# Two mixers reordered: hgrn ahead of attention's projections, output gates late

## The chip, the cores and the metric

One core of one Trainium2 chip. The metric is the device time of one execution in microseconds (us). Times in the profile count from the first instruction of the profiled execution.

## The reference

Two transformer blocks on 512 tokens of width 1024, in float32. The change touches the first block's two layers and a helper that the second block's attention also uses. Each layer of the first block is `x + gate * mixer(norm(x))`, then a SwiGLU. The mixer, cut to what matters:

```
proj = h @ w_in                                   # 1024 -> 2824
out_a = sliding_window_attention(rope(norm(aq)), rope(norm(ak)), av, sinks)       # 8 heads, window 128
out_b = rmsnorm(hgrn2_chunked(bq, log_f(bf), bv)) * silu(bg)                      # gated recurrence, 4 heads
out_c = rmsnorm(gated_delta_chunked(cq, ck, cv, beta, g)) * silu(cg)              # delta net, 4 heads
mixed = concat(out_a, out_b, out_c) @ w_out
```

`aq`, `ak`, ... are slices of `proj`; `cq`, `ck`, `cv` pass a causal convolution of width 4 and a silu first. A vector of modulations, `silu(c) @ ada_w + ada_b`, gives scale, shift and gate of each layer.

## The kernel before, in words

**Order of the work.** The kernel is traced as one straight program. A planner then lays out the queue of each engine by a timeline of its own, in which program order is the priority: work named earlier goes first where both could run. Tiles of one tag share a fixed number of buffers, and buffers are given in program order: a tile waits for the release of the one whose place it takes. Semaphores are put in by the planner. `after` (line 280) adds an order of issue between two instructions, without a wait.

**ScalarE's tables.** `act` (line 263) keeps track of the function table: Exp and Ln share one, Silu has another. When the next function in program order needs the other table, it loads it at that point (line 270), ordered behind all uses of the table before it. So all Exp and Silu uses keep their program order by groups.

**Generators.** Each part of a mixer is a generator that yields between pieces; `run` runs generators to their ends one after the other, `mix` interleaves them by counts, `islice(g, n)` runs n pieces, `track` sets the group of tiles and the PSUM tag of `psm`. This order of naming is the priority. Matrix products go through `mm` (line 297), transposes through `tr` (line 301), activations through `act` (line 274), so most instructions carry these lines, and tiles tell them apart.

**PSUM.** Each mixer has eight banks: two each of tags pd (projections, heads and scores of attention), pg (delta net, transposed probabilities of attention), po (modulation, accumulated values of attention, output rows of the delta net), ph (hgrn).

**A mixer** (function `mixers` in `build`, from line 2090): `mixer` projects keys, values and gate inputs; `gdn_gates` prepares the delta net's decays; `gdn_proj` projects `qT`, `kT`, `vT` with convolution and Silu, then the delta net's output gate `sg` (256 columns by tokens, `gen_tok`) and hgrn's output gate `hg` (256 columns, `run_cm`). Then `run` names, in this order:

- `gdn`: the delta net (`gen_gdn`, line 899). Norms (`csq`, `ln`), decay masks, `AT` and `QK`, an inverse by doubling (`T`, `TT`, `Y`, `Ah`), `kbg`, `kd`, `vb`, `U`, `WT`, a scan of 8 chunks (`St`, `VN`), the output `O`, its norm (`oms`), the product with `sg` (two POOL multiplications and `om`) and transposes into `gout`.
- `ap`: attention's query projection `aq`, two loads of 256 columns. `hp`: hgrn's `hz`, `hq`, `hv`, three loads. A load is 1 MB of weights, split into a high and a low part (ScalarE copies, VectorE subtracts), three matmuls per 128 rows.
- `ada` (layer 0 only): modulations 2 to 5, each four loads of 1 MB and 32 matmuls into one po bank, then transposes in another.
- attention (`gen_attn`, line 1262): squares and rms norm (Ln, Exp in `rsqrt_s`), rope, heads transposed (`gen_heads`), then scores of four blocks (`sm`, `nm`, `den`) mixed with values (`gen_values`, line 1342). The first 18 pieces come alone; the rest is mixed two to one with `part`, the output rows 6 and 7 (those of the delta net) into po.
- `hg_(0)`, `hg_(1)`: hgrn (`gen_hgrn`, line 1103) for two halves of the channels: gates with Exp and Ln (`he`, `lf`), a cumulated sum, seven levels of `ed` against masks into `hW`, the output `hO`, its norm (`hsq`, with Ln and Exp) and the product with `hg`.

Behind the mixer, `mixed` splits the outputs and runs the remaining output rows through `gen_out`.

**Values** (`gen_values`): per key block, probabilities of two groups of four heads are transposed into PSUM, the first group copied by VectorE, the second by ScalarE into `PT`, then two products into the two halves of one po bank:

```
if G:
    self.act(T[G], p)
else:
    self.nc.vector.tensor_copy(T[G], p)
...
for G in range(2):
    g = slice(G * 64, G * 64 + 64)
    self.mm(po[g], V[:, g], T[G], s == 0, s == len(keys) - 1)
```

The third mixer (`even`) calls the same function, with pd, po and pn as banks and six keys in each of four blocks.

Of the kernel before, what the change touches and what calls it, by code (L numbers as in the profile page):

```python
# [168 lines left out]
class Net:  # L169
# [662 lines left out]
    def gdn_proj(self, l, X, Wv):  # L832

        self.grp, self.pg = "G", "pg"
        conv = self.P(f"conv{l}").rearrange("p (c j) -> p c j", j=4)
        qkv = [self.pair([128, 2, 512], n) for n in ("qT", "kT", "vT")]

        def fin(c, p):
            y = self.t([128, 512], "cy")
            self.act(y, p, AF.Copy, scale=conv[:, c, 3:4])  # L840
            for s in (1, 2, 3):
                self.stt(y[:, s:], p[:, :512 - s], conv[:, c, 3 - s:4 - s], y[:, s:], OP.mult, OP.add)
            self.act(qkv[c // 2][:, c % 2], y, AF.Silu)

        self.run_cm(Wv, 1792, 768, X, fin)
        sg = self.pair([128, 2, 2, 4, 64], "sg")

        def fg(b, p):
            v = p.rearrange("p (j h e) -> p h j e", j=2, h=2)
            for hh in range(2):  # L850
                self.act(sg[:, hh, :, b, :], v[:, hh], AF.Silu)

        self.run_tok(X, 4, (Wv[:, :, 2560:2816],), fg)
        self.grp = "P"
        hg = self.pair([128, 2, 512], "hg")
        self.run_cm(Wv, 1536, 256, X, lambda c, p: self.act(hg[:, c], p, AF.Silu))
        return qkv, sg, hg

# [39 lines left out]

    def gen_gdn(self, l, qkv, sg, gates, out):
        nc, g = self.nc, self.nc.gpsimd  # L900
        lb, G, rest, gl = gates
        qT, kT, vT = qkv
# [153 lines left out]
        for hh in range(2):  # L1056
            d = slice(hh * 64, hh * 64 + 64)
            p = self.psm().rearrange("p (u e) -> p u e", e=64)
            for u in range(8):
                q, b = divmod(u, 4)  # L1060
                for j in range(2):
# [4 lines left out]
        yield from sysmm(QK, Pair([v.rearrange("p q b e -> p (q b) e") for v in VN.t]),  # L1066
                         lambda hh, p: self.tt(O[:, hh], O[:, hh], p, OP.add))

        ms = self.t([128, 16], "oms")
        for hh in range(2):  # L1070
# [21 lines left out]
    def gen_hgrn_proj(self, X, Wv, out):  # L1092
        pr = lambda n: self.pair([128, 2, 512], n)
        z, q, vT = pr("hz"), pr("hq"), pr("hv")
        cp = lambda t: (lambda c, p: self.act(t[:, c], p))
        for c0, fn in ((1024, cp(z)), (768, cp(q)), (1280, cp(vT))):
            yield from self.gen_cm(Wv, c0, 256, X, fn)
        out += [z, q, vT]

# [242 lines left out]
    def gen_values(self, b, keys, den, out, pt, pv, py):  # L1342

        po = self.psm(pv)
        for s, (P, o, V) in enumerate(keys):
            T = []
            for G in range(2):
# [4 lines left out]
                if G:  # L1352
                    self.act(T[G], p)
                else:
                    self.nc.vector.tensor_copy(T[G], p)
            for G in range(2):
                g = slice(G * 64, G * 64 + 64)
                self.mm(po[g], V[:, g], T[G], s == 0, s == len(keys) - 1)
            yield
# [681 lines left out]
def build(nc, tc, a, cwhere, pwhere):  # L2041
    with ExitStack() as ctx:
# [20 lines left out]
        for l in range(2):  # L2063
            with ExitStack() as st:
# [25 lines left out]
                def mixers(out, Wov):  # L2090
# [3 lines left out]
                    gates = n.gdn_gates(l, gates)  # L2094
                    qkv, sg, hg = n.gdn_proj(l, X, Wv)
                    proj, qt = [], []
                    T = n.track
                    gdn = T(n.gen_gdn(l, qkv, sg, gates, out), "G", "pg")
                    hp = T(n.gen_hgrn_proj(X, Wv, proj), "P", "pg")
                    ap = T(n.gen_attn_proj(X, Wv, qt), "A", "pg")  # L2100
                    ada = T(chain(*[n.gen_ada_pe(a['ada_w'][0], q, [(c1, n.P('ada_b0'), mods[0])], 'po') for q in (2, 3, 4, 5)]), "A", "pg") if l == 0 else iter(())

                    def hg_(c):
                        yield from T(n.gen_hgrn(l, c, proj + [hg], out), "I", "ph")

# [10 lines left out]
                    part = T(chain(halve(), n.gen_out(Wov, slice(6, 8), Z, col(mods[l], 2), "po", False, 8)), "A", "pg")  # L2116
                    n.run(gdn, ap, hp, ada, chain(islice(at, 18), n.mix((at, 2), (part, 1))), hg_(0), hg_(1))
                    return 6
# [103 lines left out]
```

## Time and profile before

| what | value |
|---|---|
| runs | 3109.3, 3103.52, 3100.19 us; median 3103.52 |
| profiled execution | 3102.67 us, span from first to last instruction 3100.9 us |
| TensorE (PE) busy | 2921.0 us, 94% |
| VectorE (DVE), ScalarE (ACT), GpSimd (POOL) busy | 1422.8, 894.8, 361.4 us |
| granted TensorE clock, mean | 0.949 |
| chain that ended last | PE 85%, DVE 9%, ACT 2%, issue 2%, DMA 1% |

How to read it: PE is busy 94% of the span, so a view of the whole tells little. The granted clock says at which share of its full speed TensorE ran: in each moment one of two levels, 1.0 (2.4 GHz) or 0.5 (1.2 GHz), so a mean between them is a mixture. A matmul at half clock counts as busy for longer. An instruction's `<-` shows which tiles it reads; `[x <-y]` behind a row is idle time of its engine and what ended it.

### The profile page before, as it was taken

The page shows a single profiled execution, that of the slowest core. Times are in us where ns is not written, and L with a number is a line of the kernel's source. Part 1 is how long each engine was busy: PE and PEld are TensorE (multiplying, and loading weights), DVE is VectorE, ACT ScalarE, POOL GpSimd, SP SyncE. Part 2 cuts the span into 40 slices and gives each one's busy share as a digit, 9 for nine tenths or more (in the row PEclk, how much of TensorE's full clock was granted, in tenths as well). Part 3 has the DMA queues.
Part 4 walks back from the last instruction along what each step waited for, and adds up shares of the span by engine and source line. Part 5 has one row for each costly group of instructions (what it writes and reads, how often), then busy time and mean ns, then how long its engine had stood idle before and what let it go on. Part 6 is the DMA issues. An engine that isn't in the chain of part 4 may idle for free.

```text
span 3100.9 us, 42214 instructions
## 1 busy us (share of the span) xinstructions
PE 2921.0 (94%) x17403; PEld 1958.3 (63%) x17403; DVE 1422.8 (46%) x2688; ACT 894.8 (29%) x1716; POOL 361.4 (12%) x284
## 2 busy tenths in 40 slices
PE   7998999999999899999999899899999988999998
PEld 5875578888887667888899744534434474344343
DVE  4346566564546659689545754311111362211112
ACT  4333343233433343423344344211101222011011
POOL 0212111011023202213001300100000011000000
PEclk9996899999999699999999899899999998999998
DMA  6233156563220036599412000899999729999995
GB/s 219 69 119 125 35 151 185 174 188 87 91 65 17 5 102 199 157 300 312 127 58 69 21 21 8 334 409 409 409 409 409 270 83 360 409 389 394 409 409 214
DMA packets 334401, 636.98 MB, mean 205 GB/s; under 512 B 16640, under 2 KB 204288, under 8 KB 334208
## 3 DMA queue, kind: packets, MB, share of 16 engines
q1 hardware_dynamic: 332128, 634.15, 56.4%
q8 instruction: 137, 2.24, 0.3%
q14 instruction: 56, 0.46, 0.0%
q10 hardware_dynamic: 2080, 0.13, 0.0%
HBM read 632.14 MB, written 2.10 MB: 205 GB/s over the span
## 4 chain that ended last, share of the span: by engine, by line
PE 85%; DVE 9%; ACT 2%; issue 2%; DMA 1%; POOL 0%; DVEq 0%; POOLq 0%; ACTq 0%
PE pd L297 41%; PE pm L297 18%; PE pa L297 8%; PE po L297 4%; PE pg L297 4%; PE pe L297 3%; PE pd L301 2%; PE ph L297 2%; DVE aacc L294 1%; PE pn L297 1%; DVE x L294 1%; PE pg L301 1%; DMA raw<-ada_w 1%; DVE rt L285 1%; DVE split L285 1%
## 5 line engine op out<-in xcount | busy, mean ns | idle before, releaser
L297 PE MATMUL pd<-X,split 128*128 128x512 f32 x2640 | 629.8, 394 | 11.4 <-ACT X L274 6.9
L297 PEld LDWEIGHTS pd<-X,split 128*128 128x128 f32 x2640 | 493.4, 189 | 121.6 <-ACT X L274 10.0
L297 PE MATMUL pm<-rawx,xs 128*64 128x512 f32 x1440 | 403.4, 600 | 0.7 <-ACT xs L274 0.5
L297 PEld LDWEIGHTS pm<-rawx,xs 128*64 128x64 f32 x1440 | 126.1, 136 | 190.4 <-issue 180.0
L297 PE MATMUL pa<-rawx,maT 128*64 128x512 f32 x728 | 202.6, 600 | 7.6 <-ACT maT L274 7.6
L274 ACT ACTIVATE split<-raw 128x1024 fp32r<-128x1024 f32 (+5 forms) x164 | 141.9, 871 | 195.6 <-PE pd L297 129.3
L285 DVE TENSOR_TENSOR split<-raw,split 128x1024 fp32r<-128x1024 f32 (+4 forms) x135 | 150.8, 1122 | 87.1 <-ACT split L274 86.2
L297 PE MATMUL pd<-split,X 128*128 128x256 f32 x1296 | 180.1, 293 | 9.4 <-ACT split L274 6.1
L297 PEld LDWEIGHTS pd<-split,X 128*128 128x128 f32 x1296 | 165.3, 195 | 16.0 <-ACT split L274 6.2
L297 PE MATMUL pd<-X,splitx 128*128 128x512 f32 x720 | 173.7, 391 | 0.0
L297 PEld LDWEIGHTS pd<-X,splitx 128*128 128x128 f32 x720 | 135.6, 189 | 29.3
L297 PE MATMUL pd<-aH,split 128*128 128x512 f32 x484 | 153.4, 389 | 0.0
L294 DVE SCALAR_TENSOR_TENSOR x<-pd,modl,x 128x512 f32<-128x512 f32 x136 | 96.5, 746 | 99.5 <-PE pd L297 99.4
L294 DVE SCALAR_TENSOR_TENSOR yL<-pa,gv,yH 128x512 fp32r<-128x512 f32 x32 | 24.0, 750 | 246.5 <-ACT yH L274 246.5
L297 PEld LDWEIGHTS pa<-rawx,maT 128*64 128x64 f32 x728 | 66.6, 137 | 107.5 <-issue 95.9
L1974 DVE COPY gv<-pd 64x1 f32<-64x1 f32 x32 | 5.0, 156 | 272.7 <-PE pd L297 272.5
L285 DVE TENSOR_TENSOR ms<-ms,pm 128x512 f32<-128x512 f32 x32 | 22.0, 688 | 227.5 <-issue 186.9
L294 DVE SCALAR_TENSOR_TENSOR aacc<-rawx,cs_c,aacc 128x512 f32<-128x512 f32 x148 | 125.4, 888 | 0.0
L285 POOL TENSOR_TENSOR aL<-sg,aH 128x512 fp32r<-128x512 f32 x44 | 66.8, 1518 | 398.3 <-ACT aH L274 398.3
L297 PEld LDWEIGHTS pd<-aH,split 128*128 128x128 f32 x484 | 90.9, 188 | 19.4
L274 ACT ACTIVATE split<-rawx 128x1024 fp32r<-128x1024 f32 (+3 forms) x64 | 59.5, 934 | 150.8 <-PE pd L297 122.2
L297 PE MATMUL pm<-raw,xs 128*64 128x512 f32 x272 | 101.5, 597 | 0.0
(683 smaller groups left out, 4738.8 us busy)
## 6 DMA issues: line engine op xcount, KB each, us to landing
rawx<-w_exp_gate SPq DMA_DIRECT2D x94, 1024.0 KB, 14.5
rawx<-w_exp_down SPq DMA_DIRECT2D x91, 1024.0 KB, 12.5
rawx<-w_exp_up SPq DMA_DIRECT2D x86, 1024.0 KB, 17.6
raw<-ada_w SPq DMA_DIRECT2D x30, 1024.0 KB, 5.2
rawx<-w_mod SPq DMA_DIRECT2D x29, 1024.0 KB, 5.4
raw<-w_in SPq DMA_DIRECT2D x22, 1024.0 KB, 5.1
raw<-w_exp_up SPq DMA_DIRECT2D x20, 1024.0 KB, 16.7
raw<-w_mod SPq DMA_DIRECT2D x19, 1024.0 KB, 5.4
```

The costliest lines, as they stand in the source:

```text
L274: i = self.nc.scalar.activation(out, in_, f, **k)
L285: return (eng or self.nc.vector).tensor_tensor(out, a, b, op)
L294: return self.nc.vector.scalar_tensor_tensor(out, a, s, b, op0, op1)
L297: return self.nc.tensor.matmul(out, l, r, start=start, stop=stop, skip_group_check=True)
L301: return self.nc.tensor.transpose(out, x, self.C("ident")[0:k, 0:k])
L1974: nc.vector.tensor_copy(gv[64 * i:64 * i + 64], pg[64 * i:64 * i + 64, i:i + 1])
```

## The change

hgrn's projections take in `hg`, and stand with hgrn's first half right behind the delta net; then come attention's projections, then the gate `sg`, the first 14 pieces of attention, the end of the delta net (`gen_gdn_end`, cut out of `gen_gdn`), then hgrn's second half, the rest of attention and the modulations mixed one to two to two, and the output rows `part` last. In `gen_values` the first product is ordered behind the second group's copy.

```diff
--- before.py
+++ after.py
@@ -843,18 +843,19 @@
             self.act(qkv[c // 2][:, c % 2], y, AF.Silu)
 
         self.run_cm(Wv, 1792, 768, X, fin)
+        return qkv
+
+    def gen_gdn_gate(self, X, Wv, got):
+
         sg = self.pair([128, 2, 2, 4, 64], "sg")
+        got.append(sg)
 
         def fg(b, p):
             v = p.rearrange("p (j h e) -> p h j e", j=2, h=2)
             for hh in range(2):
                 self.act(sg[:, hh, :, b, :], v[:, hh], AF.Silu)
 
-        self.run_tok(X, 4, (Wv[:, :, 2560:2816],), fg)
-        self.grp = "P"
-        hg = self.pair([128, 2, 512], "hg")
-        self.run_cm(Wv, 1536, 256, X, lambda c, p: self.act(hg[:, c], p, AF.Silu))
-        return qkv, sg, hg
+        yield from self.gen_tok(X, 4, (Wv[:, :, 2560:2816],), fg)
 
     def gdn_gates(self, l, gates):
 
@@ -896,7 +897,7 @@
                 self.act(gl[q, j], v(p[:, 32 + 16 * j:48 + 16 * j])[q, hh], AF.Exp)
         return lb, G, rest, gl
 
-    def gen_gdn(self, l, qkv, sg, gates, out):
+    def gen_gdn(self, l, qkv, gates, got):
         nc, g = self.nc, self.nc.gpsimd
         lb, G, rest, gl = gates
         qT, kT, vT = qkv
@@ -1065,7 +1066,11 @@
             yield
         yield from sysmm(QK, Pair([v.rearrange("p q b e -> p (q b) e") for v in VN.t]),
                          lambda hh, p: self.tt(O[:, hh], O[:, hh], p, OP.add))
-
+        got.append(O)
+
+    def gen_gdn_end(self, l, O, sg, out):
+
+        nc, g = self.nc, self.nc.gpsimd
         ms = self.t([128, 16], "oms")
         for hh in range(2):
             sq = self.t([128, 8, 64], "osq")
@@ -1093,9 +1098,10 @@
         pr = lambda n: self.pair([128, 2, 512], n)
         z, q, vT = pr("hz"), pr("hq"), pr("hv")
         cp = lambda t: (lambda c, p: self.act(t[:, c], p))
-        for c0, fn in ((1024, cp(z)), (768, cp(q)), (1280, cp(vT))):
+        hg = pr("hg")
+        for c0, fn in ((1024, cp(z)), (768, cp(q)), (1280, cp(vT)), (1536, lambda c, p: self.act(hg[:, c], p, AF.Silu))):
             yield from self.gen_cm(Wv, c0, 256, X, fn)
-        out += [z, q, vT]
+        out += [z, q, vT, hg]
 
     def gen_hgrn(self, l, c, proj, out):
 
@@ -1350,12 +1356,14 @@
                     self.tr(p[:, j * 128:j * 128 + 128], P[4 * G + j][:, o:o + 128])
                 T.append(self.t([128, 512], "PT"))
                 if G:
-                    self.act(T[G], p)
+                    second = self.act(T[G], p)
                 else:
                     self.nc.vector.tensor_copy(T[G], p)
             for G in range(2):
                 g = slice(G * 64, G * 64 + 64)
-                self.mm(po[g], V[:, g], T[G], s == 0, s == len(keys) - 1)
+                i = self.mm(po[g], V[:, g], T[G], s == 0, s == len(keys) - 1)
+                if G == 0:
+                    self.after(i.ins, second.ins)
             yield
         r = self.t([128, 8], "rden")
         self.nc.vector.reciprocal(r, den)
@@ -2092,16 +2100,20 @@
                     if l == 0:
                         n.consts("a", n.m)
                     gates = n.gdn_gates(l, gates)
-                    qkv, sg, hg = n.gdn_proj(l, X, Wv)
-                    proj, qt = [], []
+                    qkv = n.gdn_proj(l, X, Wv)
+                    proj, qt, O, sg = [], [], [], []
                     T = n.track
-                    gdn = T(n.gen_gdn(l, qkv, sg, gates, out), "G", "pg")
-                    hp = T(n.gen_hgrn_proj(X, Wv, proj), "P", "pg")
-                    ap = T(n.gen_attn_proj(X, Wv, qt), "A", "pg")
+                    gdn = T(n.gen_gdn(l, qkv, gates, O), "G", "pg")
+                    hp = T(n.gen_hgrn_proj(X, Wv, proj), "P", "pd")
+                    ap = T(n.gen_attn_proj(X, Wv, qt), "A", "pd")
+                    sp = T(n.gen_gdn_gate(X, Wv, sg), "G", "pd")
                     ada = T(chain(*[n.gen_ada_pe(a['ada_w'][0], q, [(c1, n.P('ada_b0'), mods[0])], 'po') for q in (2, 3, 4, 5)]), "A", "pg") if l == 0 else iter(())
 
                     def hg_(c):
-                        yield from T(n.gen_hgrn(l, c, proj + [hg], out), "I", "ph")
+                        yield from T(n.gen_hgrn(l, c, proj, out), "I", "ph")
+
+                    def end():
+                        yield from T(n.gen_gdn_end(l, O[0], sg[0], out), "G", "pg")
 
                     BANKS = "pg", "po", "po"
                     at = T(n.gen_attn(l, qt, kv, out, BANKS), "A", "pd")
@@ -2114,7 +2126,7 @@
                             yield
 
                     part = T(chain(halve(), n.gen_out(Wov, slice(6, 8), Z, col(mods[l], 2), "po", False, 8)), "A", "pg")
-                    n.run(gdn, ap, hp, ada, chain(islice(at, 18), n.mix((at, 2), (part, 1))), hg_(0), hg_(1))
+                    n.run(gdn, hp, hg_(0), ap, sp, islice(at, 14), end(), n.mix((hg_(1), 1), (at, 2), (ada, 2)), part)
                     return 6
 
                 mixed(a["w_out"][l], col(mods[l], 2), mixers)
```

## Rows read from the trace of the kernel before

**Rows 1.** Busy time by stretch: start:end, length, PE, PEld, DVE, ACT, POOL, clock, DMA.

```profile
86.60:206.80 120.20, 119.71 (x1482) 104.12 (x1481) 46.91 (x65) 39.66 (x73) 27.93 (x24) 1.00 0.19 63
206.80:319.70 112.90, 95.82 (x1188) 63.41 (x1187) 71.76 (x232) 38.53 (x87) 27.95 (x29) 0.71 0.41 139
319.70:390.60 70.90, 67.70 (x401) 37.16 (x399) 35.40 (x119) 28.01 (x79) 5.34 (x7) 0.85 0.12 38
...
854.60:979.10 124.50, 119.61 (x1419) 103.65 (x1418) 65.26 (x129) 42.63 (x81) 36.82 (x31) 0.99 0.15 48
979.10:1062.10 83.00, 68.75 (x1093) 57.76 (x1092) 57.53 (x167) 33.22 (x74) 20.86 (x22) 0.68 0.02 5
1062.10:1123.90 61.80, 59.30 (x401) 33.48 (x399) 35.20 (x119) 27.60 (x79) 5.35 (x7) 0.90 0.13 43
1807.40:1928.50 121.10, 118.73 (x501) 52.18 (x500) 52.63 (x126) 50.26 (x143) 6.34 (x5) 0.97 0.04 14
```

**Rows 2.** Timeline of PE in the inverse of layer 0: start, length, instruction.

```profile
169.91 2.08 PE L297 MATMUL pg<-Y,TT 64*64 64x64 f32 x64
171.93 2.79 PE L297 MATMUL pd<-X,split 128*128 128x512 f32 x11
```

**Rows 3.** Timeline of ACT, end of the input projections of layer 0.

```profile
90.90 0.63 ACT L274 ACTIVATE vT<-cy 128x512 f32<-128x512 f32 x1 [2.50 <-DVE cy L294]
...
114.22 1.28 ACT L270 ACT_TABLE_LOAD   x1
115.51 0.74 ACT L274 ACTIVATE ln<-pg,cst_g 128x8 f32<-128x8 f32 x4
```

**Rows 4.** Timeline of DVE, scores and first value copy of layer 1.

```profile
1005.33 0.35 DVE L1317 CUSTOM_DVE_ANT_0 sm<-pd,cst_a,prm 128x128 f32<-128x128 f32 x1 [1.41 <-PE pd L297]
...
1062.08 0.68 DVE L1355 COPY PT<-pg 128x512 f32<-128x512 f32 x1
1062.68 0.48 DVE L1317 CUSTOM_DVE_ANT_0 sm<-pd,cst_a,prm 128x256 f32<-128x256 f32 x1
```

**Rows 5.** Tiles he and hO, layers 0 and 1: ns min/median/max, first to last start.

```profile
L294 DVE SCALAR_TENSOR_TENSOR he<-hz x2: 685/688/692, 159.9 to 285.4; 128x512 f32<-128x512 f32 x2
L274 ACT ACTIVATE hsq<-hO x2: 630/631/632, 285.2 to 367.6; 128x512 f32<-128x512 f32 x2
...
L294 DVE SCALAR_TENSOR_TENSOR he<-hz x2: 683/684/684, 928.0 to 1023.5; 128x512 f32<-128x512 f32 x2
L274 ACT ACTIVATE hsq<-hO x2: 629/630/630, 1023.2 to 1105.9; 128x512 f32<-128x512 f32 x2
```

**Rows 6.** Tiles ass and sm, layers 0 and 1: attention's Ln and scores.

```profile
L274 ACT ACTIVATE rsy<-ass x1: 236/236/236, 229.1 to 229.1; 128x40 f32<-128x40 f32 x1
L1317 DVE CUSTOM_DVE_ANT_0 sm<-pd,cst_a,prm x32: 345/479/484, 269.1 to 380.1; 128x256 f32<-128x256 f32 x24, 128x128 f32<-128x128 f32 x8
...
L274 ACT ACTIVATE rsy<-ass x1: 220/220/220, 929.3 to 929.3; 128x40 f32<-128x40 f32 x1
L1317 DVE CUSTOM_DVE_ANT_0 sm<-pd,cst_a,prm x32: 329/476/485, 990.6 to 1114.7; 128x256 f32<-128x256 f32 x24, 128x128 f32<-128x128 f32 x8
```

**Rows 7.** Tile sg, layer 0: the gate of the delta net.

```profile
L274 ACT ACTIVATE sg<-pd x8: 271/274/278, 91.8 to 103.0; 128x128 f32<-128x128 f32 x8
...
L285 POOL TENSOR_TENSOR sg<-sg,prm x2: 1318/1805/2292, 103.2 to 104.5; 128x512 f32<-128x512 f32 x2
```

**Rows 8.** DMA issues of the whole run, weight loads of 1 MB: count, KB each, us to landing.

```profile
raw<-ada_w SPq DMA_DIRECT2D x30, 1024.0 KB, 5.2
```

**Rows 9.** Timeline of PE in the third mixer: value products, split and together.

```profile
1820.24 1.07 PE L297 MATMUL po<-PT,V 128*64 128x512 f32 x2
...
1853.82 1.08 PE L297 MATMUL po<-PT,V 128*64 128x512 f32 x4
```

**Rows 10.** Groups by line, PE: value products, layer 1 from 979.1, third mixer.

```profile
L297 PE MATMUL po<-PT,kv 128*64 128x512 f32 x28 | 12.5, 681 | 0.0
...
L297 PE MATMUL po<-PT,V 128*64 128x512 f32 x96 | 47.7, 616 | 0.1
```

## The prediction

> **What bounds the kernel now.** I cut the time into stretches first, by the table of engine busy times, because the average hides them [rows 1]. In each of the first two mixers there is a dense stretch, a thin one and a tail. Dense: 86.6 to 206.8 us in layer 0, where TensorE is busy 119.71 of 120.20 us at a granted clock of 1.00 (its upper level, 2.4 GHz), and 854.6 to 979.1 in layer 1. Thin: from the moment the projections run out to the first attention values, 206.8 to 319.7 and 979.1 to 1062.1, with clocks of 0.71 and 0.68, a mixture of both levels. The tail is the rest, at 0.85 and 0.90. I call "loss" a stretch's length minus busy time times clock. Thin: 112.9 - 95.82 x 0.71 = 44.9 us, and 83.0 - 68.75 x 0.68 = 36.2. Tails: 13.4 and 8.4. The matrix work is the same before and after except for one edit, so a gain in the mixers must come out of this loss: 103 us in all, 81 of them thin.
>
> Why the dense stretch is dense shows in TensorE's timeline: a step of the delta-net inverse takes 2.08 us, and 2.79 us of projection instructions lie between it and the next [rows 2]. The chain of dependent steps costs nothing while projections last. Afterwards the delta-net scan, attention and hgrn all wait on evacuations, and the clock falls.
>
> Two more things set the order. On ScalarE the last Silu of the delta-net's input is at 90.90, but its first Ln only at 115.51, behind a table load at 114.22 that the code orders behind all Silu uses, those of both output gates too [rows 3]. And attention's scores stop at 1005.3 and go on at 1062.68, directly behind the first copy of transposed probabilities [rows 4]: that copy needs a pg bank, and banks go round in the order the program names them, so it stands behind the delta-net's last output. Scores of the next block stand behind it in their own tiles.
>
> **The change, part by part.**
>
> *Delta net.* Without the gates in front, its Ln can follow the table load right behind 90.90 + 0.63: some 23 us earlier. PE is full there anyway, so this alone gains nothing; it takes the delta net's end out of the way of the values.
>
> *hgrn's first half.* Its four projections now precede attention's, so its work falls into the dense stretch. Before, it began at 159.9 and its last square was at 285.2 [rows 5], mostly in the thin stretch. Its matmuls lengthen the dense stretch by what they take out of the thin one: zero in the sum, but done at full clock.
>
> *Attention.* Its projections come after hgrn's, and its Ln/Exp now waits on ScalarE for the delta-net gate's Silu, which waits for hgrn's first half. Queued behind it are the second hgrn half and the rest of attention. In layer 1 the Ln was at 929.3 [rows 6], inside the dense stretch; now it comes after it. What must run from the end of the projections to the first values: the gate, 8 x 0.274 = 2.2 us [rows 7]; two table loads, 2.6; norm, rope and heads, from the Ln at 229.1 to the first score at 269.1, 40.0 us; scores of block 0, 990.6 to 1005.7, 15.1 [rows 4, 6]. Together 60 us, in place of 112.9 and 83.0. Beside it run the second hgrn half and the delta-net end, the kind of work that was there before, so I keep the loss per us: 44.9/112.9 = 0.40 and 36.2/83.0 = 0.44. New loss 24 and 26; gain 21 + 10 = **31 us**. The ends: if the second half and the delta net fill it so that the rate halves, 25 more; if the thin stretch keeps its lengths, nothing. I take the middle because the 40.0 us was measured with that kind of neighbour.
>
> *Table loads.* Four more per mixer, 1.28 us each [rows 3]; two are counted above, the others lie on a ScalarE that is busy 39.66 of 120.2 us: nothing, and 5 us in all if that cover is gone. The row shows an activation right behind the load. The Trainium skill's page ScalarE: Activation LUTs (What ACT_TABLE_LOAD costs) counts a drain too, 2.66 us a switch, and its rule for kernel authors is to finish one set before switching, which speaks against this change. By the page, estimated, the time would be some 5 us higher.
>
> *Gate work.* The two POOL multiplications of the gate, 1.8 us each [rows 7], move from an idle POOL into the rope's neighbourhood; the delta-net end has slack against the scores, so nothing, at worst 4 us a mixer.
>
> *Weight loads.* SP issues the same seven 1 MB projection loads in another order; a load of that size lands in 5.2 us [rows 8], and feeds 48 instructions of TensorE at some 0.25 us each [rows 2], so they stay hidden. The 16 loads of the modulation (layer 0) now stand behind all of them and run beside the values. There it shares two po banks with the values in program order, and each of three quarters is 4 x 5.2 us of loads. A value block that meets a quarter unfinished waits: 0 to 9 us, estimated; the tail has other work, so I take **2 us lost**.
>
> *Output rows of the delta net* go behind attention: the same TensorE work, late instead of early in a tail that is already 95% busy: nothing, at most 4 us either way.
>
> *Paired value matmuls.* The first of the two value products is now ordered behind the copy that the second needs, so the two become neighbours in the queue; this queues the next key's transposes behind both. Split, a product of two instructions takes 1.07 us; where both stand together, four take 1.08 [rows 9]. This helper also serves the third mixer, which the trace shows full (118.73 of 121.1 us at 0.97). There 96 such instructions, 24 keys, take 47.7 us [rows 10]; all paired, 24 x 1.08 = 25.9, so up to 21.8 us less. In layer 1, 12.5 us for seven keys against 7.6: 4.9; the same in layer 0: 10 together. But the edge orders issue only: if the first product starts before the second's copy has landed, they overlap in part. Between zero and everything I take half, since already paired keys stand in the same trace beside split ones: **11 + 5 us**.
>
> **Sum.** 31 - 2 + 11 + 5 = 45. The profiled execution took 3102.67 us (span 3100.9), 0.85 below the median of the runs, 3103.52; 3102.67 - 45 = 3057.7, so 3058 to be held against the median.
>
> **The rivals.**
>
> *Slower: hgrn's first half holds ScalarE.* The gate's Silu, with it attention's Ln and the second hgrn half, cannot pass hgrn's last Exp. I put hgrn's start at about 150 (its gate is the eighth of eight groups that fill about 0.6 of TensorE's time) and the end of the projections at about 228. If it took 125 us as before (159.9 to 285.2) [rows 5], the gate would come at 275, 47 us late; in layer 1, by the 95 us from 928.0 to 1023.2 and the same starts 768 us later, 17 late. 64 - 45 = +19: 3122. It decides from 78 us on. Against it: before, it had attention and the modulation as neighbours and waited for its own projections. The Trainium skill's rule of finishing one set before switching (ScalarE: Activation LUTs, Rules for kernel authors) would have kept both gates together. Chance 0.13.
>
> *The order changes, the loss does not.* The queues are laid out by a planner's own timeline, with program order only as priority. If attention's late start costs what the earlier hgrn saves (layer 1 starts its rope 70 us later), only the pairing is left: 3103 - 16 = 3087; with less pairing it falls within no change. For it: layer 1, where I find only 10 us. Chance 0.24.
>
> **How the numbers follow.** Forecast 0.63, slower 0.13, pairing only 0.24. Low end: half the thin loss again (25) and some more pairing (8) below the forecast, 3025. High end: the second rival with half its pairing, 3096; beyond it lies little but the slower case. A measurement here tells some 0.3% (9.3 us) from no change. Faster by more: 0.63 less 0.03 for mis-sized terms, plus 0.19 of the second rival, 0.79. Within: 0.08. Slower: 0.13.
>
> **What would show it.** Right: Ln of the delta net some 23 us earlier; hgrn's first Exp before 160 and its last before the end of the projections; attention's Ln within 5 us behind the gate's Silu; the half-clock stretch ahead of the values some 60 us long in both layers; value products in groups of four, 1.1 us each, and the third mixer shorter by about 10 us. Wrong: the gate's Silu waiting on ScalarE for hgrn with TensorE idle; values waiting for a po bank behind the modulation; a third mixer of the same length; a layer 1 that ends later than 1124 us less what layer 0 gained.

## The result, and the profile after

The changed kernel takes 3141.53 us, the median of 4 runs (3137.05 to 3144.22); the kernel before, run beside it, 3104.68. The ratio is 1.0117 [1.0097, 1.0137]: 36 us slower where 45 faster were forecast. A ratio leaves out executions more than 1.5% above the shortest of their kernel, which only e13 below has, four of twelve. The profiled execution has a span of 3142.4 us at a mean granted clock of 0.941 (before: 3100.9 and 0.949).

Stages first, in the table of windows of the changed kernel (start:end and length in us, then busy time of PE, PEld, DVE, ACT, POOL with counts, granted clock, DMA share, GB/s). Four rows belong to layer 0 (dense, thin up to the first values, tail, output rows of the delta net), four to layer 1, one to the third mixer.

```profile
86.60:229.00 142.40, 138.96 (x2105) 122.34 (x2104) 72.18 (x140) 54.22 (x93) 32.31 (x29) 1.00 0.16 50
229.00:294.60 65.60, 40.34 (x467) 29.17 (x465) 47.11 (x154) 22.17 (x56) 24.93 (x23) 0.73 0.21 73
294.60:386.00 91.40, 81.66 (x452) 37.44 (x452) 28.68 (x110) 27.71 (x83) 1.64 (x3) 0.69 0.36 124
386.00:400.00 14.00, 11.94 (x54) 9.37 (x54) 9.63 (x17) 5.68 (x12) 4.43 (x6) 1.00 0.38 116
863.80:1009.00 145.20, 143.54 (x2093) 125.54 (x2092) 74.10 (x141) 56.24 (x96) 31.81 (x30) 0.98 0.13 42
1009.00:1072.70 63.70, 36.48 (x337) 29.67 (x336) 42.18 (x136) 20.93 (x51) 21.04 (x20) 0.62 0.02 5
1072.70:1150.20 77.50, 74.40 (x444) 39.84 (x445) 33.30 (x126) 28.00 (x84) 3.62 (x4) 0.68 0.00 1
1150.20:1163.00 12.80, 11.39 (x46) 7.97 (x44) 9.03 (x14) 4.29 (x11) 5.33 (x6) 1.00 0.32 102
1848.50:1969.50 121.00, 118.62 (x501) 54.10 (x500) 53.61 (x126) 49.97 (x143) 6.35 (x5) 0.96 0.04 14
```

Against [rows 1]: the thin stretches came out as long as forecast, 65.6 and 63.7 us. But with loss taken as in the prediction (length minus busy time times clock), they lose 65.6 - 40.34 x 0.73 = 36 us and 63.7 - 36.48 x 0.62 = 41, where 24 and 26 were forecast: TensorE is busy for little more than half of each. The tails lose 91.4 - 81.66 x 0.69 = 35 and 77.5 - 74.40 x 0.68 = 27 us where they lost 13.4 and 8.4, and 14.0 and 12.8 us of output rows follow. By the starts of `rstd`, the next norm, layer 0's mixer ends at 436.0 us (before 426.7), and layer 1's takes 388.3 us from its own norm on (before 357.3): 9 + 31 us. The third mixer, from its first gate `gt` to the MoE's `gv`, takes 453.4 us in both.

**The hole.** ScalarE's timeline at the end of layer 1's projections (start, length, operation; in brackets idle time before it and what ended it):

```profile
1009.26 0.45 ACT L274 ACTIVATE sg<-pd 128x128 f32<-128x128 f32 x2 [1.58 <-PE pd L297]
1010.69 0.45 ACT L274 ACTIVATE sg<-pd 128x128 f32<-128x128 f32 x2 [0.99 <-PE pd L297]
1025.24 0.63 ACT L274 ACTIVATE osq<-O 128x512 f32<-128x512 f32 x1 [14.10 <-DVE O L285]
...
1029.58 0.45 ACT L274 ACTIVATE sg<-pd 128x128 f32<-128x128 f32 x2 [1.07 <-PE pd L297]
1031.58 0.45 ACT L274 ACTIVATE sg<-pd 128x128 f32<-128x128 f32 x2 [1.56 <-PE pd L297]
1032.05 1.28 ACT L270 ACT_TABLE_LOAD   x1
1033.34 0.24 ACT L274 ACTIVATE rsy<-ass 128x40 f32<-128x40 f32 x1
...
1033.59 0.61 ACT L274 ACTIVATE he<-he 128x512 f32<-128x512 f32 x1
```

and TensorE's beside it and from there on:

```profile
1025.14 1.97 PE L297 MATMUL pg<-VN,QK 64*64 64x64 f32 x32
1027.04 4.51 PE L297 MATMUL pd<-split,X 128*128 128x256 f32 x22
...
1049.07 1.94 PE L301 MATMUL pg<-cst_g,om 128*128 128x128 f32 x8 [17.53 <-DVE om L285]
1055.47 0.69 PE L301 MATMUL pd<-cst_g,kk 128*128 128x128 f32 x2 [4.46 <-ACT kk L274]
```

The gate's last Silu is held by its own products on TensorE, half of which (`pd<-split,X`) come behind the delta net's last products (`pg<-VN,QK`). Behind it, 0.25 us apart, start attention's Ln and the second hgrn half's Exp. Nothing that could feed TensorE is ready: attention's norm and rope, the delta net's end and the first steps of hgrn all go through VectorE, whose three costliest groups from 1032.7 to 1052.7 (busy us, mean ns, idle before) are

```profile
L285 DVE TENSOR_TENSOR aq<-aq,ass 128x512 f32<-128x512 f32 x4 | 6.8, 1690 | 0.0
L285 DVE TENSOR_TENSOR kv<-kv,ass 128x128 f32<-128x128 f32 x4 | 2.8, 688 | 0.0
L285 DVE TENSOR_TENSOR om<-O,sg 128x256 f32<-128x256 f32 x4 | 2.5, 679 | 0.0
```

Layer 0 has the same hole; its window is

```profile
244.60:264.60 20.00, 2.44 (x18) 2.27 (x17) 16.40 (x36) 5.42 (x14) 13.54 (x12) 0.61 0.00 1
```

**What follows it.** Layer 1 of the changed kernel in steps of 20 us, the values beginning at 1072.7:

```profile
1032.70:1052.70 20.00, 1.94 (x8) 1.57 (x8) 18.03 (x49) 4.97 (x12) 13.53 (x13) 0.54 0.04 13
1052.70:1072.70 20.00, 15.23 (x111) 11.09 (x111) 16.43 (x68) 12.26 (x30) 6.74 (x7) 0.67 0.00 1
1072.70:1092.70 20.00, 20.00 (x121) 11.35 (x121) 8.42 (x31) 6.86 (x23) 2.65 (x3) 0.50 0.00 1
1092.70:1112.70 20.00, 20.00 (x107) 10.43 (x105) 9.05 (x36) 6.20 (x19) 0.97 (x1) 0.50 0.00 1
1112.70:1132.70 20.00, 20.00 (x145) 11.18 (x144) 7.30 (x28) 5.24 (x17) 0.00 (x0) 0.83 0.00 1
```

and four such steps of the kernel before, where the values begin at 1062.1:

```profile
1022.10:1042.10 20.00, 13.60 (x119) 9.84 (x121) 15.04 (x39) 8.44 (x14) 4.17 (x4) 0.50 0.00 1
1042.10:1062.10 20.00, 14.84 (x239) 12.45 (x237) 17.01 (x41) 7.39 (x15) 7.82 (x8) 0.67 0.01 2
1062.10:1082.10 20.00, 20.00 (x126) 10.86 (x124) 10.62 (x41) 6.95 (x22) 2.44 (x3) 0.70 0.00 1
1082.10:1102.10 20.00, 20.00 (x166) 12.21 (x164) 9.22 (x33) 7.93 (x25) 2.18 (x3) 1.00 0.16 53
```

TensorE was busy 1.94 us of 20 where it had been busy 13.60, and the values then ran at the lower clock (1.2 GHz) for over 40 us instead of some 12 (20 us at a mean of 0.70, by the two levels). A row with PE 20.00 of 20.00 at a clock of 0.50 is not a full TensorE but the same products taking longer: a value product (`po<-PT,kv`) lasts 1082 ns on average from 1072.7 to 1119 us, 618 ns behind that. That the half clock follows the hole in time does not make the hole its cause; e4, e6 and e14 below speak against that. The Trainium skill (TensorE: Matmul & The Clock Gate, What's actually happening) says that the throttled clock is the default and that activity releases it. The row of the hole, at 0.54, agrees; the two rows from 1072.7 on, busy throughout and still at 0.50, do not show activity alone releasing it, and here the measurement stands.

### The profile page after: what moved, and what is told of

It is laid out like the page before. It is cut to its first block, busy times and chain, and to the rows that moved or that the text cites. A ratio compares the mean times of both kernels' runs of the same rounds, so it can differ in the third digit from the quotient of the medians.

```text
span 3142.4 us, 42246 instructions
## 1 busy us (share of the span) xinstructions
PE 2930.6 (93%) x17403; PEld 1960.5 (62%) x17403; DVE 1427.2 (45%) x2688; ACT 903.5 (29%) x1724; POOL 362.8 (12%) x284
## 4 chain that ended last, share of the span: by engine, by line
PE 86%; DVE 8%; ACT 2%; DMA 2%; issue 1%; POOL 0%; DVEq 0%; SPq 0%; ACTq 0%; POOLq 0%
PE pd L297 41%; PE pm L297 18%; PE pa L297 8%; PE pg L297 4%; PE pe L297 4%; PE po L297 4%; PE ph L297 2%; PE pd L301 2%; DVE aacc L294 1%; PE pn L297 1%; DVE x L294 1%; PE pg L301 1%; DMA raw<-ada_w 1%; DVE rt L285 1%; DVE aq L285 0%
## 5 line engine op out<-in xcount | busy, mean ns | idle before, releaser
L297 PE MATMUL pd<-split,X 128*128 128x256 f32 x1296 | 186.9, 296 | 9.1 <-ACT split L274 6.5
```

What stands on the lines that cost most here:

```text
L297: return self.nc.tensor.matmul(out, l, r, start=start, stop=stop, skip_group_check=True)
```

## The experiments

Each kernel was also profiled, in one execution. The layers' columns are read from the starts of `rstd`, as above: where layer 0's mixer ends, and how long layer 1's is.

| kernel | median us | ratio to before | layer 0 | layer 1 |
|---|---|---|---|---|
| before (in its first runs) | 3103.52 | | 426.7 | 357.3 |
| after | 3141.53 | 1.0117 [1.0097, 1.0137] | 436.0 | 388.3 |
| e1 pairing alone | 3100.77 | 0.9977 [0.9963, 0.9991] | 419.9 | 358.4 |
| e2 after, no pairing | 3141.65 | 1.0110 [1.0094, 1.0126] | 441.5 | 382.0 |
| e3 after, rows mid | 3134.20 | 1.0088 [1.0071, 1.0106] | 448.9 | 368.6 |
| e4 after, modulation early | 3126.83 | 1.0075 [1.0062, 1.0088] | 427.0 | 385.5 |
| e5 after, gate ahead of hgrn | 3127.26 | 1.0071 [1.0057, 1.0085] | 433.2 | 373.3 |
| e6 = e3 and e4 | 3091.82 | 0.9976 [0.9960, 0.9992] | 408.8 | 366.5 |
| e7 after, gate first | 3133.56 | 1.0095 [1.0081, 1.0110] | 429.3 | 388.0 |
| e8 = e6 and e7 | 3075.98 | 0.9912 [0.9893, 0.9931] | 388.6 | 364.4 |
| e9 = e8, hgrn's gate first too | 3068.27 | 0.9878 [0.9854, 0.9902] | 393.8 | 357.2 |
| e10 = e8, no pairing | 3101.25 | 0.9984 [0.9964, 1.0003] | 404.6 | 372.3 |
| e11 = e8, layer 1 as before | 3069.12 | 0.9889 [0.9866, 0.9913] | 396.8 | 358.4 |
| e12 = e8, useless products in layer 1 | 3088.56 | 0.9951 [0.9933, 0.9970] | 398.5 | 374.6 |
| e13 before, rows last | 3130.98 | 1.0040 [1.0008, 1.0073] | 445.8 | 385.5 |
| e14 = e13, modulation late | 3135.64 | 1.0099 [1.0067, 1.0131] | 438.8 | 358.5 |
| e15 before, hgrn's first half first | 3080.48 | 0.9935 [0.9917, 0.9953] | 403.7 | 354.2 |

Layer 0 of e8, e11 and e12 is named in the same order and took 388.6 to 398.5 us: a single profile tells no less than some 10 us there. The profiled execution can also lie off the median: e8's by 11 us, e1's by 9, e15's by 7 and e14's by 17, all below it. The changed kernel's line, to which the edits below are made, is

```
n.run(gdn, hp, hg_(0), ap, sp, islice(at, 14), end(), n.mix((hg_(1), 1), (at, 2), (ada, 2)), part)
```

### Pairing: e1 and e2

e1 puts the edit of `gen_values` alone into the kernel before; e2 takes it alone out of the kernel after:

```diff
-                i = self.mm(po[g], V[:, g], T[G], s == 0, s == len(keys) - 1)
-                if G == 0:
-                    self.after(i.ins, second.ins)
+                self.mm(po[g], V[:, g], T[G], s == 0, s == len(keys) - 1)
```

> The kernel before with one edit of the change alone: the first value product is ordered behind the second copy of transposed probabilities. Forecast of the prediction (half of all pairable keys): 16 us less in all, 11 of them in the third mixer (its start to the start of the MoE values before: 1566.1 to 2019.5 = 453.4 us, forecast 442). Rival theory, from the trace of after, where the third mixer took 453.4 us again although its value products fell from 47.7 to 39.9 us of busy time: the edit only trades product time for waits of the scores, so 0 to 3 us either way in all three mixers. A third possibility: it costs in the first two mixers (each 2 to 8 us longer) and so carries part of the 37 us by which the change is slower.

> The changed kernel without the pairing edit. If the new order of the mixers carries the whole loss: within 5 us of the changed kernel (3141.5), so still about 1.01 of the kernel before, third mixer 453 us long. If the pairing carries part of it: 10 us or more below the changed kernel, the tails of the first two mixers (values start to last ao, after: 294.6 to 386.0 and 1072.7 to 1150.2) shorter by 5 us each or more.

Alone it gives 0.0023 x 3103 = 7 us, by the profile in layer 0 (less than two profiles can tell apart there); in the changed kernel nothing. It is not what makes the change slower. In the third mixer the groups of instructions (busy us, mean ns, idle before) are, before:

```profile
L297 PE MATMUL pe<-X 64*128 64x512 f32 x52 | 18.1, 643 | 1.7 <-ACT eP L274 1.7
```

and after:

```profile
L297 PE MATMUL po<-PT,V 128*64 128x512 f32 x96 | 39.9, 636 | 0.0
...
L297 PE MATMUL pe<-X 64*128 64x512 f32 x52 | 27.1, 686 | 1.7 <-ACT eP L274 1.7
```

The values' 96 products fell from 47.7 [rows 10] to 39.9 us, and the 52 score products rose from 18.1 to 27.1 with unchanged idle time: a single score product lasts nearly as long as before (686 ns for 643), so they overlap less. What the values' products gained by standing together, the scores lost: the mixer is as long as before.

### Output rows and modulation: e3, e4, e6

e3 mixes `part` into attention again, e4 names `ada` ahead of attention, e6 does both (the added lines in this order):

```diff
-n.run(gdn, hp, hg_(0), ap, sp, islice(at, 14), end(), n.mix((hg_(1), 1), (at, 2), (ada, 2)), part)
+n.run(gdn, hp, hg_(0), ap, sp, islice(at, 14), end(), n.mix((ada, 2), (hg_(1), 1), (chain(islice(at, 4), n.mix((at, 2), (part, 1))), 3)))
+n.run(gdn, hp, hg_(0), ap, sp, ada, islice(at, 14), end(), n.mix((hg_(1), 1), (at, 2)), part)
+n.run(gdn, hp, hg_(0), ap, sp, ada, islice(at, 14), end(), n.mix((hg_(1), 1), (chain(islice(at, 4), n.mix((at, 2), (part, 1))), 3)))
```

> The changed kernel, with the delta net's output rows again mixed into the attention from its fourth step on instead of behind it. Theory A (the tail lost its filler: full-array products of the output rows kept TensorE busy and its clock up beside the values; now they run alone at the end for 12 us and the tail falls to half clock): each mixer 10 to 25 us shorter than in the changed kernel, clock of the tail back towards 0.85, total 3141 - 20 to - 45. Theory B (the tail is long because the second hgrn half falls into it, late on ScalarE behind the gate): at most 5 us per mixer, clock of the tail stays below 0.75. Theory C (layer 0's tail is long because the modulation runs beside the values on shared banks): layer 0 stays within 5 us, layer 1 can gain.

> The changed kernel with the modulation (layer 0 only) again ahead of the attention's blocks. Theory C (values of layer 0 wait on banks that they share with the modulation, 277 to 373 us): layer 0's mixer 10 to 20 us shorter than in the changed kernel (436.0 us to the next norm), layer 1 unchanged (388.3). Rival: the modulation was not in the way; at most 5 us, since layer 1 has no modulation and its tail is as long (77.5 + 12.8 us against 91.4 + 12).

> Output rows mixed into the attention as before, and the modulation ahead of it. Theory A (output rows are the tail's filler) with the reading that in layer 0 the rows had to wait for the modulation's columns when only they were moved (layer 0 448.9 us there, 13 more than in the changed kernel, layer 1 368.6, 20 less): layer 0 now 436 - 20 = 416 us, layer 1 369 again, total 3141 - 40 = 3101. Rival: layer 0 does not gain from its rows (its values end late because of the second hgrn half): 430 us or more, total 3115 or more.

Layer 1 has no modulation, so there e3 and e6 both move only rows (attention keeps two pieces a round, but for its first four): 19.7 us less against after, 19.0 against e4. Layer 0 gains only when both are moved. The reason that I expected, rows waiting for the modulation's columns, is not what e3 shows: its first row is added at 327.4 us, as early as e6's (327.9). But rows, values and modulation there share the two po banks, and the modulation's last product starts at 398 us instead of after's 373.5. The windows of layer 1, values and then the stretch up to the next norm, of e4:

```profile
1060.20:1139.10 78.90, 76.47 (x445) 40.95 (x446) 33.45 (x126) 27.69 (x84) 3.43 (x4) 0.65 0.00 1
1139.10:1188.60 49.50, 46.18 (x205) 36.66 (x203) 27.27 (x35) 16.37 (x29) 5.32 (x6) 1.00 0.47 143
```

and of e6:

```profile
1042.40:1115.40 73.00, 71.00 (x460) 40.27 (x458) 38.50 (x130) 30.53 (x86) 7.03 (x9) 0.84 0.12 37
1115.40:1151.70 36.30, 35.10 (x160) 28.88 (x160) 19.07 (x25) 12.46 (x21) 0.00 (x0) 1.00 0.41 122
```

The rows' 13.2 us leave the end, and the values do not grow by them but shrink by 5.9, at 0.84 instead of 0.65. The hole ahead of the values is the same in both: from its last projection to the first values TensorE is busy 17.19 of 41.5 us in e4 (from 1018.7) and 18.08 of 43.7 in e6 (from 998.7). So the clock of the values does not follow from the hole alone. From after to e4 and on to e6 the medians fall by 15 and 35 us.

### The gates: e5, e7, e8, e9

```diff
-n.run(gdn, hp, hg_(0), ap, sp, islice(at, 14), end(), n.mix((hg_(1), 1), (at, 2), (ada, 2)), part)
+n.run(gdn, hp, sp, hg_(0), ap, islice(at, 14), end(), n.mix((hg_(1), 1), (at, 2), (ada, 2)), part)
+n.run(sp, gdn, hp, hg_(0), ap, islice(at, 14), end(), n.mix((hg_(1), 1), (at, 2), (ada, 2)), part)
+n.run(sp, gdn, hp, hg_(0), ap, ada, islice(at, 14), end(), n.mix((hg_(1), 1), (chain(islice(at, 4), n.mix((at, 2), (part, 1))), 3)))
+n.run(sp, hq, gdn, hp, hg_(0), ap, ada, islice(at, 14), end(), n.mix((hg_(1), 1), (chain(islice(at, 4), n.mix((at, 2), (part, 1))), 3)))
```

The added lines are e5, e7, e8 and e9; `hq` is the projection and Silu of `hg`, cut out of `hp`.

> The changed kernel, with the delta-net gate (4 groups of products, its Silu) laid ahead of the first hgrn half instead of behind attention's projections. Theory B (the gate's late Silu holds ScalarE, with it attention's Ln and the second hgrn half): gate's last Silu before 170 in layer 0 and 60 us or more earlier in layer 1, second hgrn half out of the tail, each mixer 10 to 20 us shorter, total 3141 - 20 to - 40. Theory A (output rows missing in the tail): thin stretch may shrink, but the tail keeps its clock below 0.75 and its length within 8 us, total at most 10 us less. Rival to both: the gate ahead delays hgrn's first half and with it all that follows; no gain or a loss.

> The changed kernel with the delta-net gate laid ahead of the delta net itself, beside the input's Silu uses, as in the kernel before (with the gate between hgrn's projections and its first half it gave 2.8 us in layer 0 and 15 in layer 1, its Silu at 193 to 224 us still behind the delta net on TensorE). Theory B: gate done by 105 us, attention's Ln and second hgrn half start 20 to 40 us earlier, layer 0 20 us shorter (416), layer 1 15 to 25 shorter (363 to 373). Theory A: the tail keeps its half clock and its 12 us at the end; layer 0 within 8 us of 436, layer 1 no better than 373.

> All three undone at once; what is left of the change is hgrn's first half ahead of attention's projections, the delta net's end placed among the attention, the second half beside it, and the pairing. If the two causes add (20 us for the rows, 15 to 20 for the gate, in each layer): layer 0 398 to 405, layer 1 350 to 353, total 3141 - 35 - 37 = 3065 to 3075, faster than the kernel before by over 1%, and the thin stretch gives what the prediction forecast of it. If they are the same loss seen twice (whichever fills the tail): layer 0 416, layer 1 365, total about 3098, no better than the kernel before.

> The last kernel (gate first, output rows among the attention, modulation ahead of it; 3076 us, layer 0 388.6, layer 1 364.4) with hgrn's gate laid first as well, so that all Silu uses stand together as in the kernel before and fewer table loads follow. If table loads on ScalarE's path cost: one load and its way back at 1.28 us each, in the dense stretch, is nothing; at most 3 us faster per mixer. Rival: nothing within 3 us, or slower because hgrn's gate products are taken from the fill of the delta net's inverse.

While the rows stay last, the gate's place gives 14 us (e5, where its Silu came at 193 to 224 us of layer 0, not before 170) or 8 (e7); neither cures it, and e7 leaves layer 1 as long as it was, against what the theory of the late gate expected. The hole stays too where no late gate stands in front of attention's Ln: layer 1 of e7, with its gate done by 874 us, and of e8 (last row):

```profile
1016.70:1026.70 10.00, 5.15 (x54) 4.18 (x51) 10.00 (x23) 1.72 (x3) 9.33 (x8) 0.50 0.00 0
1026.70:1036.70 10.00, 2.22 (x34) 2.03 (x36) 9.85 (x38) 1.05 (x2) 5.23 (x6) 0.50 0.01 2
...
974.60:994.60 20.00, 6.96 (x73) 5.80 (x75) 19.85 (x55) 2.98 (x5) 13.63 (x13) 0.50 0.00 0
```

There VectorE (third of the busy times) is all but full. The late Silu sets when the hole comes, not that there is one. With rows and modulation back, the place of the gate gives another 16 (e6 to e8), nearly all in layer 0, so the causes add in layer 0 only. e9, with 20 table loads like the kernel before (e8: 24, after: 28), is the fastest kernel of the study, 37 us below the kernel before, but its interval overlaps e8's: a cost of the loads is not shown.

### Layer 1: e10, e11, e12

e10 is e8 without the pairing. e11 names layer 1 as the kernel before does (`n.run(sp, hq, gdn, end(), ap, hp, chain(islice(at, 18), n.mix((at, 2), (part, 1))), hg_(0), hg_(1))`). e12 computes layer 0's modulation once more in layer 1:

```diff
+waste = n.t([128, 48], "waste")
-ada = T(chain(*[n.gen_ada_pe(a['ada_w'][0], q, [(c1, n.P('ada_b0'), mods[0])], 'po') for q in (2, 3, 4, 5)]), "A", "pg") if l == 0 else iter(())
+ada = T(chain(*[n.gen_ada_pe(a['ada_w'][0], q, [(c1, n.P('ada_b0'), mods[0] if l == 0 else waste)], 'po') for q in (2, 3, 4, 5)]), "A", "pg")
```

> The 3076 us kernel without the pairing edit. Pairing alone on the kernel before gave 7 us (0.9977), of them 7 in layer 0, -1 in layer 1 and 1.5 in the third mixer; taken out of the changed kernel it cost 5.5 in layer 0 and gave 6 in layer 1. If the pairing harms layer 1: layer 1 358 here instead of 364, layer 0 some 394, third mixer 452, total within 5 us of 3076. If it helps everywhere: total 3083, layer 1 364 or more.

> Layer 0 in the order of the 3076 us kernel, layer 1 in the order of the kernel before (delta net whole, then attention's projections, hgrn's, attention with the rows, both hgrn halves), pairing kept. If the order of layer 1 carries its 7 us (364.4 against 357.3, and 358.4 with the pairing alone): layer 0 389, layer 1 358, total 3070, the best of all. Rival: the layers differ for another reason and layer 1 stays at 364, total 3076.

> The 3076 us kernel, with useless work added: in layer 1 the modulation's products, loads and evacuations of layer 0 (four quarters, 64 wide products) are computed once more, in the same place of the order, into a tile that nobody reads; the outputs are not touched. Theory D (layer 0 gained 38 us and layer 1 lost 7 because layer 0's thin stretch holds the modulation's products, which keep TensorE from running dry and its clock at 1.00 there, while in layer 1 TensorE was busy 6.96 of 20 us at 974.6 to 994.6 and the clock stayed at 0.50 until 1042): layer 1 shorter in spite of 64 more wide products, by 10 to 30 us, its tail at 0.95. Rival E (layer 0 gained for its own reasons, its modulation had been in the way before): layer 1 longer by the added work, 10 us or more (64 products of some 0.14 us at full clock, and 16 loads of 5.2 us).

Pairing, worth nothing in the changed kernel, is worth 25 us by the medians beside the better order (e10 against e8), by the profiles 16 in layer 0 and 8 in layer 1: my expectation missed. e11 came as expected, level with e9. In e12 the filler did not pay. Its windows up to the values and beside them:

```profile
1017.00:1050.20 33.20, 32.43 (x299) 20.79 (x299) 18.37 (x62) 16.13 (x41) 8.59 (x9) 0.68 0.45 149
1050.20:1113.30 63.10, 59.66 (x324) 32.97 (x324) 33.75 (x114) 27.57 (x82) 4.41 (x6) 0.87 0.14 43
```

The values took 63.1 us instead of e8's 70.2, at 0.87 instead of 0.81, but began 17 us later in the layer; layer 1 became 10 us longer. Length minus busy time times clock, from the last projections to the end of the values, fell from 49 us in e8 to 39, so the filler did keep some clock up; the work that was added cost more. The theory falls as a way to gain with useless work.

### One part at a time on the kernel before: e13, e14, e15

```diff
-n.run(gdn, ap, hp, ada, chain(islice(at, 18), n.mix((at, 2), (part, 1))), hg_(0), hg_(1))
+n.run(gdn, ap, hp, ada, at, hg_(0), hg_(1), part)
+n.run(gdn, ap, hp, islice(at, 14), n.mix((at, 2), (ada, 2)), hg_(0), hg_(1), part)
+n.run(gdn, hp, hg_(0), ap, ada, chain(islice(at, 18), n.mix((at, 2), (part, 1))), hg_(1))
```

> The kernel before with one part of the change alone: the delta net's output rows laid behind the attention and hgrn in both mixers. Prediction: at most 4 us either way. Theory A, from the pairs of kernels that differ in this alone (layer 1 -19.7 and -19.0 us, layer 0 -18.2): the stretch from the last attention output to the next norm grows from 36.3 to 49.3 us in both layers, and the values stretch does not shrink by as much; 13 to 20 us a mixer, 26 to 40 in all, ratio 1.008 to 1.013.

> The last kernel with the modulation (layer 0) also laid beside the attention's later blocks, as in the change. Prediction's term: 2 us lost, 0 to 9. From the pair of changed kernels that differ in this alone (layer 0 427.0 against 436.0): 9 us more in layer 0, nothing in layer 1, total 9 above the kernel with the rows last. Rival: with hgrn in its old place the values are not delayed by the shared banks; within 4 us.

> The kernel before with the core of the change alone: hgrn's projections and first half ahead of attention's projections, the gates first, output rows among the attention, delta net whole, no pairing. Prediction's term: thin stretch to 60 us, 21 us gained in layer 0 and 10 in layer 1, 31 in all, ratio 0.990. From the kernel with both gates first (layer 0 393.8, layer 1 357.2, with pairing, against 419.9 and 358.4 for the pairing alone): layer 0 15 to 26 us shorter, layer 1 within 4 us, total 3085 +/- 8. If nothing remains without pairing and a late delta-net end: within 5 us of the kernel before.

The added lines are e13, e14 and e15, in the kernel before. e13's twelve runs spread from 3092.63 to 3151.34 us. By the medians the rows alone cost the kernel before 29 us (3130.98 against 3102.41), by the ratio 12; rows and late modulation together cost 31 by the ratio (e14). e13's profiled execution took 3147.44 us, e14's 3118.48, 17 below the median of its six. Layer 1 is named in the same order in both, with the rows last. Around e14's values, which begin at 1072.3:

```profile
1052.30:1072.30 20.00, 14.80 (x246) 12.65 (x247) 16.35 (x41) 7.08 (x14) 7.80 (x8) 0.68 0.01 2
1072.30:1092.30 20.00, 19.57 (x185) 11.50 (x184) 11.84 (x48) 10.03 (x30) 0.96 (x1) 1.00 0.00 1
```

There the clock rose as the values began; they took 51.1 us, and the layer 358.5, one more than before. The values of e14 and of e13, whole:

```profile
1072.30:1123.40 51.10, 48.78 (x362) 25.83 (x361) 27.99 (x109) 24.50 (x73) 0.96 (x1) 1.00 0.00 1
...
1082.90:1156.00 73.10, 71.61 (x362) 36.48 (x363) 28.55 (x109) 24.79 (x72) 0.97 (x1) 0.63 0.00 1
```

The same order cost 1 us in one execution and 28 in the other (385.5 us), without the changed kernel's hole in front. So with the rows last the tail can be as short as before, but a typical execution of e14, by its median, is 17 us longer than the one profiled, and the changed kernel, whose four runs lie within 7 us, showed no short one.

e15 gives 22 us by the medians: layer 0 23 us shorter, layer 1 3. Its thin stretches, from the last projections to the first values, layer 0 and layer 1:

```profile
236.40:306.10 69.70, 59.28 (x683) 33.95 (x683) 48.52 (x159) 23.13 (x58) 21.92 (x23) 0.83 0.62 209
...
978.00:1035.20 57.20, 39.73 (x467) 31.78 (x467) 46.87 (x156) 21.18 (x54) 22.34 (x22) 0.58 0.02 6
```

By the prediction's measure they lose 69.7 - 59.28 x 0.83 = 20 us and 57.2 - 39.73 x 0.58 = 34, against 44.9 and 36.2 before. Layer 1's is 26 us shorter and loses as much as ever (e8: 56.0 - 35.55 x 0.63 = 34 too). In layer 0 the modulation's loads (DMA 0.62) and products fall into the stretch; that they make the difference is argued, not shown.

## Why the prediction was wrong

**The step that failed first** is the sentence "Beside it run the second hgrn half and the delta-net end, the kind of work that was there before, so I keep the loss per us". That work does not feed TensorE beside attention's rope: it starts behind the same Silu and then stands in the same queue of VectorE, which was busy 18.03 of 20 us while TensorE was busy 1.94. Forecast loss of the thin stretches 24 + 26 us, measured 36 + 41: 27 of the miss. The Silu is the smaller part of it, since with the gate first the hole stays: by the same measure the thin stretches of e7 lose 33 + 37. And the loss per us cannot be kept even without the other parts: 0.40 and 0.44 were assumed, e15 has 0.29 and 0.60.

**The second** is "Output rows of the delta net [...] the same TensorE work, late instead of early in a tail that is already 95% busy: nothing, at most 4 us either way". I read 95% busy as full without asking at which clock, and kept the tails' loss at 13.4 and 8.4 us. It became 35 and 27, with 2 and 1 in the rows behind: 44 us of the miss, the larger part. Of this the rows give back about 19 us a layer when moved (e3, e6), and in the kernel before the move costs 29 us by the medians, 12 by the ratio (e13). Only in the one execution of e14 that was profiled did it cost layer 1 as little as forecast (1 us). That rows among the values keep the half clock shorter is shown; why they do is not, and the hole does not explain it alone (e4 and e6, e13 and e14).

**Modulation.** Forecast 2 us lost, 0 to 9. e4 shows 9 in layer 0, 15 by the medians: the size was taken from the wrong end. The mechanism that was named, values waiting on shared banks, fits, but e4 moves the modulation out of the tail altogether and does not test it apart.

**Pairing.** Forecast 11 us in the third mixer and 5 in the first two. Measured 7 alone, nothing in the third mixer worth the name (453.4 to 451.9 in e1), and nothing in the changed kernel. "Between zero and everything I take half" fits the value products themselves (7.8 us less); it failed by leaving out what loses its neighbour, the score products. With 27, 44 and 16, less the 2 us already forecast for the modulation, the parts come to 85 us; the forecast and the mixers' lengths are 45 + 40 = 85 apart.

**What was right.** The thin stretch's length, attention's Ln within 2 us of the gate's Silu (1031.58 to 1033.34), hgrn's first half within the dense stretch (its last Exp at 221.4 in layer 0), four more table loads per mixer at 1.28 us without visible cost. The main term without the other parts has the right sign: 31 us forecast, 22 measured in e15. That layer 0 gives 23 where 21 were forecast is partly luck, since its loss per us fell, which the sum had fixed; layer 1 gives 3 of 10. The delta net's Ln came 15 us earlier, not 23. The slower rival had the sign but not the mechanism: ScalarE sat idle for 14.10 us behind the second pair of gate Silus, waiting for the delta net; hgrn did not hold it. The second rival (the order changes, the loss does not) is refuted for the whole and for layer 0 by e15 and e6; for layer 1's thin stretch, which it named itself, it holds: 36 us before, 34 in e8 and e15.

**What stays open:** whether VectorE alone keeps layer 1's loss where it is (nothing was run with less work on it; no order tried went more than 4 us below the 357.3 of before), and what decides in a tail whether the clock comes back at once (e14) or after 40 us and more (after, e13).

## What to carry to other kernels

Work that is moved out of a stalling stretch must leave something ready in it: before counting a gain, list what waits for the same late event, and on which engine it goes on: here on VectorE, and the hole stayed when the late event was taken away. A TensorE that the profile shows 95% busy at a mixed clock has a price per missing filler that busy time does not show: multiply busy time by the clock first. Moves that look like no change of work (output rows, modulation) are worth undoing one at a time, and worth doing alone on the kernel before: there they cost 31 us together, close to the whole change's 36. Here undoing two of them and the late gate turned 36 us lost into 27 gained.

## What was not expected of the hardware

The same code may meet two clocks from run to run. With the output rows last, the kernel before ran anywhere from 3092.63 to 3151.34 us on one core, and the mean granted clock moved with it, from 0.956 (3092.63 us) to 0.932 (3151.34 us). In the profiles of e14 and e13 the values of layer 1, named in the same order, ran at 1.00 and 0.63.
